# Choosing and weighting experts: look-up moved to four PSUM banks, four splits moved to GpSimd, one row split ahead, gate row by way of DRAM

## The chip, the core and the metric

The kernel runs on one core of one Trainium2 chip. A core has TensorE (PE, matrix products into PSUM), VectorE (DVE), ScalarE (ACT), GpSimd (POOL), and SyncE (SP), whose queue issues all DMAs here. SBUF and PSUM have 128 partitions; PSUM has eight banks of 512 float32 columns per partition. The metric is the device time of one execution in microseconds (us), as the median of several runs. The change touches the last quarter of the kernel alone.

## The reference, cut to what matters

The whole model is two blocks of norms, feed-forward layers, attention and convolution on 256 tokens of 1024 channels. The change lies in the last layer, which has 16384 experts, of which each token uses 8 heads x 16:

```python
q = (hblk @ w_q).reshape(B, TB, PEER_HEADS, 2, PEER_DHALF)
s = jnp.einsum('btphd,phnd->btphn', q, subkeys).astype(jnp.float32)
v, i = lax.top_k(s, PEER_TOPK)                      # 16 of 128 rows, 16 of 128 columns per head
cand = (v[..., 0, :, None] + v[..., 1, None, :]).reshape(..., PEER_TOPK * PEER_TOPK)
cidx = (i[..., 0, :, None] * PEER_NKEYS + i[..., 1, None, :]).reshape(...)
tv, tj = lax.top_k(cand, PEER_TOPK)                 # 16 of the 256 pairs
eidx = jnp.take_along_axis(cidx, tj, axis=-1)
w = jax.nn.softmax(tv, axis=-1)
a = jax.nn.gelu(jnp.einsum('btd,btpkd->btpk', hblk, w_down[eidx]))
out = jnp.einsum('btpk,btpkd->btd', w * a, w_up[eidx])
...
x = x + ga2 * out                                   # the gate ga2: one value per channel
return _rms_norm(x, g_norm_final)
```

## The kernel before

The kernel computes all 16384 experts densely, as 128 rows of 128 ("expert e" below is one such row: 128 experts). The *first product* of expert e multiplies `w_down`'s 1024 x 128 block with the 256 tokens, and its activation (a `gelu` on ScalarE) is the row `slots[e]`, 128 x 256. The chosen experts' weights multiply these rows, with zero for what was not chosen. The *second product* multiplies each row with `w_up`'s 128 x 1024 block and adds all of them up in four banks.

Every matrix is split into a high and a low half, and a product is three matmuls (high x high, low x high, high x low): 24 matmuls for an expert of the first product (lines 298 to 300, in `mm3`), 12 for one of the second (line 1859, in `up`). The halves of a weight block come from `Stream`: a DMA on SP into one of four `raw` buffers (`load`, line 232), then in `split` a copy on ScalarE that makes the high half (line 252), then a subtraction that makes the low half, on GpSimd (line 254) or on DVE (line 256). Which of the two is a list of labels; `wdn` (all blocks of the first product) is on GpSimd, `wup` (those of the second) on DVE. The halves lie in a ring of four buffers (`Hh`, `Hl`, `hl0`, `hl1` in the last layer), and a block is split three experts ahead, when PE is done with the buffer's last block. In the trace, `X` as the input of a split is a `raw` buffer too.

Each engine works through its own queue in the order in which the program was written; nothing is reordered. That order is a loop over experts in `peer`, in which DVE's work is put between experts:

- *First stage* (expert 0 to 44). `topk` is a generator; it searches the top 16 per head on DVE (`MAX8`, `FIND_INDEX8`, `MATCH_REPLACE8`), adds pairs into `cand`, searches again, and then looks up which rows and columns were chosen (lines 1806, 1809 and 1811: compare with an iota, multiply with the index, add up; for two halves of the index and two halves of the tokens, each on 128 x 2048 columns of SBUF). Each `yield` tells its cost, and the loop puts in one expert for each 2.3 of it. Two experts later PE transposes the result (line 1666), and DVE copies it to SBUF (line 1667).
- *Second stage* (expert 45 to 127). For each token DVE makes two one-hots (line 1688 for four tokens' rows, line 1692 for a token's columns and weights), and PE multiplies them into a 128 x 128 map of weights (line 1700) in one of the banks `wb`. `place` (lines 1709 and 1711) multiplies the map of four tokens into the rows that exist, and puts it where a row does not exist yet; a later row takes its weights from there (lines 1614 and 1615, on ScalarE and DVE). `token` puts the tokens between the matmuls, evenly over the experts left.
- *Second product* (`finish`). `prep(e)` splits `slots[e]` with ScalarE and DVE (`split2`, lines 324 and 325), two experts ahead. After expert 32 `ends` loads the residual and the final norm's factors into SBUF of used rows, and makes the gate a row on all partitions: four diagonal matrices on DVE (line 1849) for each half, a product with ones on PE (line 1850), a copy (line 1851). The last experts, the residual, the norm and the output follow.

Banks before: experts go around banks 4, 5, 0, 1, 2, 3 in the first stage and around 0 to 3 in the second, where bank 4 holds the iota and banks 5, 6, 7 are `wb`. `mod(2, 0, 5)` is the gate, 128 x 8 in SBUF.

Of the kernel before, what the change touches and what calls it, by code (L numbers as in the profile page):

```python
# [8 lines left out]
F32 = mybir.dt.float32  # L9
# [180 lines left out]
class Stream:  # L190
# [45 lines left out]
    def split(self, upto):  # L236
        nc = self.nc
        while self.done < min(upto, len(self.units)):
# [5 lines left out]
            if split:  # L244
# [7 lines left out]
                nc.scalar.activation(hl[:, 0, :n], raw[:, :n], AF.Copy)  # L252
                if i in (1, 2) or label[0] == "wdn" or (label[0] == "win2f" and label[1] > 7 or label[0] == "win2r" or label[:2] == ("winf", 1) and label[2] in (0, 4, 11) or label[0] == "wout2" and label[1] < 5):
# [33 lines left out]
class Build:  # L287
# [1289 lines left out]
    def peer(self, fb):  # L1577
# [8 lines left out]
        SELT = Xf[:, 0, :768].rearrange("p (a t) -> p a t", a=3)  # L1586
        con = pp.tile([P, P], F32, name="iota")
        self.SA = self.ctx.enter_context(tc.tile_pool(name="slota", bufs=1)).tile([P, NSA * S], F32, name="slotA")
        slots = [self.SA[:, e * S:(e + 1) * S] for e in range(NSA)]
# [27 lines left out]
        with tc.tile_pool(name="topk", bufs=1) as p:  # L1617
# [29 lines left out]
            nc.sync.dma_start(con, I["con2"][:, OFF2["iota"][0]:OFF2["iota"][0] + P])  # L1647
            top = self.topk(p, con, SC, SEL)
            e = 0
# [21 lines left out]
        slots += [slotB[:, j * S:(j + 1) * S] for j in range(P - 1 - NSA)] + [Xf[:, 0, 1792:2048]]  # L1671
        self.ring = [0, 1, 2, 3]
        io = self.bank[4][:, :P]
        nc.vector.tensor_copy(io, con)
        wb = [5, 6, 7]
        SAv = self.SA.rearrange("p (e t) -> p e t", t=S)
# [18 lines left out]
        def weight(t):  # L1695
            if t >= T:
                return
            oh = ohs.pop(t)
            o = self.bank[wb[t // 4 % 3]][:, t % 4 * P:(t % 4 + 1) * P]
            nc.tensor.matmul(o, firsts[t // 4][:, t % 4], oh, start=True, stop=True)  # L1700

        def place(g, e):

            bv = self.bank[wb[g % 3]].rearrange("p (t e) -> p e t", e=P)
            ts = slice(4 * g, 4 * g + 4)
# [24 lines left out]

        rest = None
        while e < P or tok[0] < T:
            g0 = tok[0] // 4
# [8 lines left out]
            for g in range(g0, tok[0] // 4):  # L1742
                if g >= 1:
                    place(g - 1, e)
                if g == T // 4 - 1:
                    place(g, e)
            if e < P:
                rest = gelu(e, o)
                e += 1
        if rest:  # L1750
            rest()

        self.finish(slots, xd, pp)

    def topk(self, p, iota, SC, SEL):
# [43 lines left out]
        yield 1.6  # L1799
        io = iota[:, :16].unsqueeze(1).broadcast_to((P, P, 16))  # L1800
        for a in range(2):
            for t in range(2):
                eq = cand[t]
                iv = i16f[t].rearrange("p (h a) n -> p h a n", a=2)
                flat = eq.rearrange("p h k n -> p (h k) n")
                nc.vector.tensor_tensor(flat, abf[t][:, a].rearrange("p h k -> p (h k)").unsqueeze(2).broadcast_to((P, P, 16)),
                                        io, OP.is_equal)
                yield 2.3
                nc.vector.tensor_tensor(eq, eq, iv[:, :, a].unsqueeze(2).broadcast_to((P, 8, 16, 16)), OP.mult)
                yield 2.3  # L1810
                nc.vector.tensor_reduce(SEL[:, a, t], flat, axis=AX.X, op=OP.add)
                yield 2.3
                if a == 0 and t == 0:
# [9 lines left out]

    def finish(self, slots, xd, pp):
        nc, I, W = self.nc, self.I, self.W
        acc = [[self.bank[4 + 2 * t + c] for c in range(2)] for t in range(2)]
        cs = {}
        Hx = self.Hh[:, 0].rearrange("p k t -> p (k t)")
        Hf4 = [Hx[:, j * 512:(j + 1) * 512] for j in range(4)]

        def prep(e):
            c = Hf4[e % 4].rearrange("p (a t) -> p a t", a=2)
            self.split2((c[:, 0], c[:, 1]), slots[e])
            cs[e] = c

        ga = self.mod(2, 0, 5)
# [3 lines left out]
        dgs = [SA[:, 5120 + j * P:5120 + (j + 1) * P] for j in range(4)]  # L1840
# [21 lines left out]
        LATE = 4  # L1862
        prep(0)
        prep(1)
# [46 lines left out]
```

## Time and profile before

| what | us |
|---|---|
| median of 3 runs (2712.96 to 2716.12) | 2714.16 |
| the profiled execution's own time | 2713.35 |
| its span, first to last instruction | 2711.6 |
| first stage and search, about 1915 to 2055 | 140 |
| second stage, about 2055 to 2340 | 285 |
| step to the second product, about 2340 to 2352 | 12 |
| second product, about 2352 to 2697 | 345 |
| norm and output, about 2697 to 2711.6 | 14.6 |

In the profile a row names line, engine, operation, output<-inputs (buffer numbers left out), size and count. A matmul's end is modelled, so that one of 0.28 us may be followed by the next after 0.12. "Idle before" is the time in which the engine stood still, with what ended it. A DMA-issuing instruction of SP shows when it was issued, not how long the transfer took.

### The profile page before, as it was taken

The numbers are of one execution on the slowest core, as the hardware profiler recorded it, in microseconds if no ns is written. First come the engines' busy times: TensorE is split into PE (matmuls) and PEld (weight loads), VectorE is DVE, ScalarE is ACT, GpSimd is POOL, SyncE is SP. The second block draws the span as 40 slices with busy tenths as digits, with TensorE's granted clock in tenths as the row PEclk, the third lists the DMA queues.
The fourth block names the chain that finished last, engine by engine and source line by source line (L and its number), as shares of the span: only waits on it lengthen the run. The fifth ranks groups of instructions, "written<-read, shape, count | busy, mean of one in ns | idle before, by whom it ended". The sixth has DMA issues, their size and how long they took to land. (4 is left out here: it accounts for less than half of the span.)

```text
span 2711.6 us, 40950 instructions
## 1 busy us (share of the span) xinstructions
PE 2634.5 (97%) x15907; PEld 2307.1 (85%) x15907; DVE 1740.6 (64%) x3393; ACT 1088.7 (40%) x1864; POOL 506.5 (19%) x284
## 2 busy tenths in 40 slices
PE   7999999999999999999998999889989999999998
PEld 5888888688888898888978999779989999888887
DVE  4877865657776565555556656775794566655555
ACT  4322234533222232222345445544444544454554
POOL 1000010120000010000121002331797666300000
PEclk9999999999999999999999999999999999999999
DMA  6665643225565545565344665524555454566564
GB/s 265 208 192 186 200 133 115 65 94 170 186 184 198 172 138 192 189 197 187 104 145 138 193 191 169 173 72 166 170 163 172 149 149 151 160 201 197 194 194 139
DMA packets 129188, 451.40 MB, mean 166 GB/s; under 512 B 15968, under 2 KB 21088, under 8 KB 127200
## 3 DMA queue, kind: packets, MB, share of 16 engines
q1 hardware_dynamic: 128992, 448.77, 51.5%
q8 instruction: 125, 2.05, 0.3%
q14 instruction: 71, 0.58, 0.1%
HBM read 446.35 MB, written 2.10 MB: 165 GB/s over the span
## 5 line engine op out<-in xcount | busy, mean ns | idle before, releaser
L298 PE MATMUL bank<-Hh,hl 128*128 128x256 f32 (+1 forms) x1944 | 656.7, 338 | 8.8 <-ACT Hh L681 4.5
L300 PE MATMUL bank<-Hh,hl 128*128 128x256 f32 (+1 forms) x1944 | 634.2, 326 | 3.9 <-POOL hl L254 3.9
L299 PE MATMUL bank<-Hl,hl 128*128 128x256 f32 (+1 forms) x1944 | 634.7, 326 | 1.4 <-DVE Hl L684 1.2
L252 ACT ACTIVATE hl<-raw 128x1024 fp32r<-128x1024 f32 (+1 forms) x401 | 410.8, 1040 | 279.8 <-DMA raw<-in_w_dram 88.3
L256 DVE TENSOR_TENSOR hl<-raw,hl 128x1024 fp32r<-128x1024 f32 (+1 forms) x316 | 380.9, 1215 | 180.2 <-ACT hl L252 179.5
L298 PEld LDWEIGHTS bank<-Hh,hl 128*128 128x128 f32 x1944 | 369.4, 190 | 51.7 <-issue 10.3
L300 PEld LDWEIGHTS bank<-Hh,hl 128*128 128x128 f32 x1944 | 369.1, 190 | 36.0 <-POOL hl L254 4.5
L299 PEld LDWEIGHTS bank<-Hl,hl 128*128 128x128 f32 x1944 | 369.6, 190 | 32.4 <-DVE Hl L684 2.7
L532 DVE SCALAR_TENSOR_TENSOR junk<-wm,cb 128x1024 bf16<-128x1024 f32 x272 | 332.1, 1221 | 16.3 <-ACT cb L538 7.1
L635 POOL TENSOR_TENSOR nacc<-nlast,nacc 128x256 f32<-128x256 f32 (+1 forms) x56 | 60.2, 1080 | 1328.8 <-issue 834.4
L254 POOL TENSOR_TENSOR hl<-raw,hl 128x1024 fp32r<-128x1024 f32 x85 | 209.8, 2473 | 146.3 <-ACT hl L252 135.0
L298 PE MATMUL bank<-G,hl 128*128 128x512 f32 (+1 forms) x673 | 227.3, 338 | 0.0
L299 PE MATMUL bank<-G,hl 128*128 128x512 f32 (+1 forms) x673 | 226.4, 336 | 0.0
L300 PE MATMUL bank<-G,hl 128*128 128x512 f32 (+1 forms) x673 | 226.4, 336 | 0.0
L324 ACT ACTIVATE G<-silu 128x512 fp32r<-128x512 f32 (+1 forms) x88 | 51.1, 580 | 417.3 <-DVE silu L820 417.3
L1859 PE MATMUL bank<-hl,Hh 128*128 128x512 f32 x768 | 179.4, 389 | 0.0
L298 PE MATMUL bank<-Hh,hm 128*128 128x512 f32 (+1 forms) x496 | 175.4, 354 | 0.0
L299 PE MATMUL bank<-Hl,hm 128*128 128x512 f32 (+1 forms) x496 | 175.1, 353 | 0.0
L300 PE MATMUL bank<-Hh,hm 128*128 128x512 f32 (+1 forms) x496 | 175.1, 353 | 0.0
L1859 PEld LDWEIGHTS bank<-hl,Hh 128*128 128x128 f32 x768 | 144.2, 188 | 30.0
L820 DVE TENSOR_TENSOR silu<-silu,bank 128x512 f32<-128x512 f32 (+1 forms) x88 | 54.6, 621 | 179.0 <-PE bank L300 177.0
L746 DVE SCALAR_TENSOR_TENSOR X<-bank,mall,X 128x256 f32<-128x256 f32 x192 | 84.5, 479 | 125.4 <-PE bank L300 125.2
(367 smaller groups left out, 5032.6 us busy)
## 6 DMA issues: line engine op xcount, KB each, us to landing
raw<-in_w_dram SPq DMA_DIRECT2D x208, 512.0 KB, 4.2
wm<-in_wmod_dram SPq DMA_DIRECT2D x128, 512.0 KB, 4.3
X<-in_wdn_dram SPq DMA_DIRECT2D x64, 512.0 KB, 3.6
raw<-in_wdn_dram SPq DMA_DIRECT2D x64, 512.0 KB, 3.6
X<-in_wup_dram SPq DMA_DIRECT2D x64, 512.0 KB, 3.5
raw<-in_wup_dram SPq DMA_DIRECT2D x64, 512.0 KB, 3.5
raw<-in_w_dram SPq DMA_DIRECT2D x64, 448.0 KB, 3.8
wm<-in_wada_dram SPq DMA_DIRECT2D x48, 512.0 KB, 4.7
```

The costliest lines, as they stand in the source:

```text
L252: nc.scalar.activation(hl[:, 0, :n], raw[:, :n], AF.Copy)
L254: nc.gpsimd.tensor_tensor(hl[:, 1, :n], raw[:, :n], hl[:, 0, :n].bitcast(F32), OP.subtract)
L256: nc.vector.tensor_tensor(hl[:, 1, :n], raw[:, :n], hl[:, 0, :n].bitcast(F32), OP.subtract)
L298: mm(o, wh, xh, start=start, stop=False)
L299: mm(o, wh, xl, start=False, stop=False)
L300: mm(o, wl, xh, start=False, stop=stop)
L324: nc.scalar.activation(dst[0], src, AF.Copy)
L532: nc.vector.scalar_tensor_tensor(junk, w, 1.0, self.cb[c], op0=OP.mult, op1=OP.mult, accum_out=o)
L635: self.nadd.tensor_tensor(acc, last, acc, OP.add)
L746: nc.vector.scalar_tensor_tensor(x, self.bank_(b, T, half), g[:, d:d + 1], x, op0=OP.mult, op1=OP.add)
L820: nc.vector.tensor_tensor(s, s, self.bank_(bb, T), OP.mult)
L1859: nc.tensor.matmul(acc[t][n], c[:, a, ts], u[:, b, n * 512:(n + 1) * 512], start=e == 0 and a + b == 0, stop=e == P - 1 and a == 1)
```

## The change

It is four edits of the last layer.

*Look-up.* The comparison, the product and the sum of the look-up work on four PSUM banks (4 to 7), 512 columns each, where they worked on a tile of 2048 columns in SBUF; the iota is copied into bank 3 ahead of the search instead of into bank 4 after it. From there on experts go around banks 0, 1, 2, and `wb` has four banks, 4 to 7. The costs told by `yield` are 2.8 instead of 2.3.

*Splits.* The low halves of `wup` 0 to 3 go to GpSimd.

*First row.* A tile `zero` of its own takes the halves of `slots[0]`; `sides` makes them in the second stage, as soon as all tokens are placed.

*Gate.* At the layer's start the gate is written to DRAM in the order of channels; `ends` reads it back as one row on all partitions. The diagonal matrices and their products are gone.

```diff
-                if i in (1, 2) or label[0] == "wdn" or (label[0] == "win2f" ...
+                if i in (1, 2) or label[0] == "wdn" or label[0] == "wup" and label[1] < 4 or (label[0] == "win2f" ...
                     nc.gpsimd.tensor_tensor(hl[:, 1, :n], raw[:, :n], hl[:, 0, :n].bitcast(F32), OP.subtract)
...
+        zero = pp.tile([P, 512], F32R, name="zero")
+        self.gd = tc.dram_tile([1, D], F32, name="gd")
+        nc.sync.dma_start(self.gd.rearrange("o (j p) -> p (o j)", p=P), self.mod(2, 0, 5))
...
             nc.sync.dma_start(con, I["con2"][:, OFF2["iota"][0]:OFF2["iota"][0] + P])
-            top = self.topk(p, con, SC, SEL)
+            self.ring = [0, 1, 2]
+            io = self.bank[3][:, :P]
+            nc.vector.tensor_copy(io, con)
+            top = self.topk(p, io, SC, SEL)
...
-        self.ring = [0, 1, 2, 3]
-        io = self.bank[4][:, :P]
-        nc.vector.tensor_copy(io, con)
-        wb = [5, 6, 7]
+        wb = [4, 5, 6, 7]
...
+            if tok[0] == T and not early and rest is None and e > NSA:
+                early = [self.sides(zero, slots[0])]
...
         for a in range(2):
             for t in range(2):
-                eq = cand[t]
                 iv = i16f[t].rearrange("p (h a) n -> p h a n", a=2)
-                flat = eq.rearrange("p h k n -> p (h k) n")
-                nc.vector.tensor_tensor(flat, abf[t][:, a]...unsqueeze(2).broadcast_to((P, P, 16)), io, OP.is_equal)
-                yield 2.3
-                nc.vector.tensor_tensor(eq, eq, iv[:, :, a].unsqueeze(2).broadcast_to((P, 8, 16, 16)), OP.mult)
-                yield 2.3
-                nc.vector.tensor_reduce(SEL[:, a, t], flat, axis=AX.X, op=OP.add)
-                yield 2.3
+                eqs = [self.bank[4 + b] for b in range(4)]
+                flat = [eq.rearrange("p (k n) -> p k n", n=16) for eq in eqs]
+                for b in range(4):
+                    mine = abf[t][:, a, 2 * b:2 * b + 2].rearrange("p h k -> p (h k)")
+                    nc.vector.tensor_tensor(flat[b], mine.unsqueeze(2).broadcast_to((P, 32, 16)), io, OP.is_equal)
+                yield 2.8
+                for b in range(4):
+                    q = eqs[b].rearrange("p (h k n) -> p h k n", h=2, k=16)
+                    nc.vector.tensor_tensor(q, q, iv[:, 2 * b:2 * b + 2, a].unsqueeze(2).broadcast_to((P, 2, 16, 16)), OP.mult)
+                yield 2.8
+                for b in range(4):
+                    nc.vector.tensor_reduce(SEL[:, a, t, 32 * b:32 * b + 32], flat[b], axis=AX.X, op=OP.add)
+                yield 2.8
...
+    def sides(self, c, slot):
+        c = c.rearrange("p (a t) -> p a t", a=2)
+        self.split2((c[:, 0], c[:, 1]), slot)
+        return c
...
             nc.sync.dma_start(gf, I["gfin"].broadcast_to((P, D)))
-            for n in range(2):
-                b = self.bank[n]
-                for j in range(4):
-                    nc.vector.tensor_scalar(dgs[j], self.C["ident"], ga[:, 4 * n + j:4 * n + j + 1], None, op0=OP.mult)
-                    nc.tensor.matmul(b[:, j * P:(j + 1) * P], self.C["ones"], dgs[j], start=True, stop=True)
-                nc.vector.tensor_copy(gab[:, n * 512:(n + 1) * 512], b)
+            nc.sync.dma_start(gab, self.gd.broadcast_to((P, D)))
...
-        prep(0)
+        if not early:
+            prep(0)
```

The first place is DVE's queue in the look-up, where one pass (one half of the index, one half of the tokens) stands. Before, it and the next pass (`cand`, `abf` and `i16f` are tiles of SBUF):

```order
L1806 TENSOR_TENSOR cand_14971<-abf_14979,iota 128x2048
L1809 TENSOR_TENSOR cand_14971<-cand_14971,i16f_14969 128x2048
L1811 TENSOR_REDUCE SEL<-cand_14971 128x128
L1806 TENSOR_TENSOR cand_14972<-abf_14980,iota 128x2048
L1809 TENSOR_TENSOR cand_14972<-cand_14972,i16f_14970 128x2048
L1811 TENSOR_REDUCE SEL<-cand_14972 128x128
```

Now the same pass, with banks 3 (`bank_66`) and 4 to 7 (`bank_67` to `bank_70`):

```order
L1814 TENSOR_TENSOR bank_67<-abf_14983,bank_66 128x512
L1814 TENSOR_TENSOR bank_68<-abf_14983,bank_66 128x512
L1814 TENSOR_TENSOR bank_69<-abf_14983,bank_66 128x512
L1814 TENSOR_TENSOR bank_70<-abf_14983,bank_66 128x512
L1818 TENSOR_TENSOR bank_67<-bank_67,i16f_14973 128x512
L1818 TENSOR_TENSOR bank_68<-bank_68,i16f_14973 128x512
L1818 TENSOR_TENSOR bank_69<-bank_69,i16f_14973 128x512
L1818 TENSOR_TENSOR bank_70<-bank_70,i16f_14973 128x512
L1821 TENSOR_REDUCE SEL<-bank_67 128x32
L1821 TENSOR_REDUCE SEL<-bank_68 128x32
L1821 TENSOR_REDUCE SEL<-bank_69 128x32
L1821 TENSOR_REDUCE SEL<-bank_70 128x32
```

Three operations of four times the columns have become twelve, and none has two inputs in SBUF any more.

The second place is DVE's queue at the end of the second stage. Before, from the first split of the second product (line 256) to the first row's halves:

```order
L256 TENSOR_TENSOR Hh<-X,Hh 128x1024
L1688 TENSOR_TENSOR X<-bank_67,X 128x512
L1692 TENSOR_SCALAR oh<-bank_67,X 128x128 x3
L1615 TENSOR_TENSOR slotB<-bank_66,slotB 128x244
L1709 TENSOR_TENSOR slotA<-slotA,bank_69 128x68x4
L1709 TENSOR_TENSOR slotB<-slotB,bank_69 128x57x4
L256 TENSOR_TENSOR Hl<-X,Hl 128x1024
L1692 TENSOR_SCALAR oh<-bank_67,X 128x128
...
L256 TENSOR_TENSOR hl_77<-raw_75,hl_77 128x1024
L1615 TENSOR_TENSOR slotB<-bank_64,slotB 128x256
L1615 TENSOR_TENSOR X<-bank_65,X 128x256
L325 TENSOR_TENSOR Hh<-slotA,Hh 128x256 x2
```

Now, from the last products of weights with rows on:

```order
L1618 TENSOR_TENSOR slotB<-bank_65,slotB 128x248
L1712 TENSOR_TENSOR slotA<-slotA,bank_69 128x68x4
L1712 TENSOR_TENSOR slotB<-slotB,bank_69 128x58x4
L1712 TENSOR_TENSOR slotA<-slotA,bank_70 128x68x4
L1712 TENSOR_TENSOR slotB<-slotB,bank_70 128x58x4
L325 TENSOR_TENSOR zero<-slotA,zero 128x256
L1618 TENSOR_TENSOR slotB<-bank_63,slotB 128x256
L1618 TENSOR_TENSOR X<-bank_64,X 128x256
L325 TENSOR_TENSOR Hh<-slotA,Hh 128x256 x2
L256 TENSOR_TENSOR Hh<-X,Hh 128x1024
```

The splits of line 256 are gone from between the one-hots, the first row's half stands ahead of the activations of the last two experts, and the first split on DVE is that of `wup` 4.

On PE the order has 48 matmuls more ahead of the transposes of the look-up's result, so two experts have moved from the second stage to the first.

## Rows read from the trace of the kernel before

**Rows 1.** Busy time by stage: stretch; PE, PEld, DVE, ACT, POOL; clock; DMA share; GB/s.

```profile
1915.00:2055.00 140.00, 133.06 (x1107) 131.42 (x1108) 119.90 (x420) 66.98 (x97) 129.77 (x45) 1.00 0.56 169
...
2055.00:2340.00 285.00, 284.40 (x2435) 284.23 (x2434) 174.37 (x500) 141.29 (x376) 191.51 (x80) 1.00 0.49 150
...
2352.00:2438.00 86.00, 86.00 (x381) 71.20 (x380) 49.67 (x64) 42.38 (x62) 0.00 (x0) 1.00 0.61 194
```

**Rows 2.** Timeline of ScalarE: start, duration, line, operation [idle before]; three of 45 activations.

```profile
1976.74 0.38 ACT L1611 ACTIVATE slotA<-bank 128x256 f32<-128x256 f32 x1 [0.73 <-PE bank L300]
...
1999.46 0.38 ACT L1611 ACTIVATE slotA<-bank 128x256 f32<-128x256 f32 x1 [1.54 <-PE bank L300]
...
2033.82 0.39 ACT L1611 ACTIVATE slotA<-bank 128x256 f32<-128x256 f32 x1 [2.70 <-PE bank L300]
```

**Rows 3.** Timeline of GpSimd beside the look-up.

```profile
2008.54 2.39 POOL L254 TENSOR_TENSOR Hh<-X,Hh 128x1024 fp32r<-128x1024 f32 x1
...
2010.90 4.43 POOL L254 TENSOR_TENSOR Hl<-X,Hl 128x1024 fp32r<-128x1024 f32 x1
...
2030.80 4.81 POOL L254 TENSOR_TENSOR hl<-raw,hl 128x1024 fp32r<-128x1024 f32 x2
```

**Rows 4.** Timeline of VectorE from the look-up to the copies of its result.

```profile
1990.76 2.27 DVE L1806 TENSOR_TENSOR cand<-abf,iota 128x2048 f32<-128x2048 f32 x1
...
1993.07 4.39 DVE L1809 TENSOR_TENSOR cand<-cand,i16f 128x2048 f32<-128x2048 f32 x1
...
2008.59 4.50 DVE L1806 TENSOR_TENSOR cand<-abf,iota 128x2048 f32<-128x2048 f32 x1
...
2031.46 4.29 DVE L1821 TENSOR_TENSOR SEL<-SEL,ss 128x128 f32<-128x128 f32 x2
...
2053.95 1.09 DVE L1667 COPY X<-bank 128x256 f32<-128x256 f32 x3 [18.20 <-PE bank L1666]
```

**Rows 5.** Groups of instructions by form, 2056 to 2352 (count, busy us, mean ns, idle before).

```profile
L254 POOL TENSOR_TENSOR hl<-raw,hl 128x1024 fp32r<-128x1024 f32 x40 | 95.8, 2396 | 44.7 <-ACT hl L252 38.4 <-PE bank L300 6.3
...
L252 ACT ACTIVATE hl<-raw 128x1024 fp32r<-128x1024 f32 x42 | 44.2, 1052 | 0.0
...
L1688 DVE TENSOR_TENSOR X<-bank,X 128x512 f32<-128x512 f32 x63 | 43.6, 692 | 88.7 <-PE bank L1700 88.7
```

**Rows 6.** Timelines of VectorE and TensorE at the step to the second product.

```profile
2339.00 1.23 DVE L256 TENSOR_TENSOR Hh<-X,Hh 128x1024 fp32r<-128x1024 f32 x1 [3.45 <-ACT Hh L252]
...
2344.35 0.28 PE L300 MATMUL bank<-Hh,hl 128*128 128x256 f32 x1
...
2346.08 0.49 PE L1700 MATMUL bank<-oh,X 128*128 128x128 f32 x2 [1.45 <-DVE oh L1692]
...
2350.16 1.19 PE L1859 MATMUL bank<-Hh 128*128 128x512 f32 x4 [0.78 <-ACT Hh L324]
...
2351.54 2.11 PE L1859 MATMUL bank<-Hh 128*128 128x512 f32 x8 [0.19 <-DVE Hh L325]
```

**Rows 7.** Timeline of TensorE around the gate's row.

```profile
2437.80 2.88 PE L1859 MATMUL bank<-Hh 128*128 128x512 f32 x12
...
2443.96 3.00 PE L1859 MATMUL bank<-Hl,Hh 128*128 128x512 f32 x12
```

**Rows 8.** Timeline of SP's queue at the layer's start and after expert 32.

```profile
1849.09 5.93 SPq L232 DMA_DIRECT2D raw<-in_wpq_dram  x2
...
1871.29 0.33 SPq L1626 DMA_DIRECT2D subk<-in_subk_dram  x1
...
2435.77 1.12 SPq L1845 DMA_DIRECT2D slotA<-in_gfin_dram  x1
```

**Rows 9.** Who waited for whom, 2352 to 2712: total us, times, longest.

```profile
ACT hl L252 <- PE bank L1859: 83.9, 62, 1.4
```

**Rows 10.** Timelines of VectorE and TensorE around expert 118's row and expert 121.

```profile
2319.18 0.38 DVE L1615 TENSOR_TENSOR slotB<-bank,slotB 128x224 f32<-128x224 f32 x1
...
2323.35 0.36 PE L298 MATMUL bank<-Hh,Hl 128*128 128x256 f32 x1
```

More of the change, by code (lines that the diff above doesn't have):

```diff
@@ L252, in split @@
                 nc.scalar.activation(hl[:, 0, :n], raw[:, :n], AF.Copy)
-                if i in (1, 2) or label[0] == "wdn" or (label[0] == "win2f" and label[1] > 7 or label[0] == "win2r" or label[:2] == ("winf", 1) and label[2] in (0, 4, 11) or label[0] == "wout2" and label[1] < 5):
+                if i in (1, 2) or label[0] == "wdn" or label[0] == "wup" and label[1] < 4 or (label[0] == "win2f" and label[1] > 7 or label[0] == "win2r" or label[:2] == ("winf", 1) and label[2] in (0, 4, 11) or label[0] == "wout2" and label[1] < 5):
                     nc.gpsimd.tensor_tensor(hl[:, 1, :n], raw[:, :n], hl[:, 0, :n].bitcast(F32), OP.subtract)
@@ L1698, in weight @@
             oh = ohs.pop(t)
-            o = self.bank[wb[t // 4 % 3]][:, t % 4 * P:(t % 4 + 1) * P]
+            o = self.bank[wb[t // 4 % 4]][:, t % 4 * P:(t % 4 + 1) * P]
             nc.tensor.matmul(o, firsts[t // 4][:, t % 4], oh, start=True, stop=True)
         def place(g, e):
-            bv = self.bank[wb[g % 3]].rearrange("p (t e) -> p e t", e=P)
+            bv = self.bank[wb[g % 4]].rearrange("p (t e) -> p e t", e=P)
             ts = slice(4 * g, 4 * g + 4)
@@ L1731, in peer @@
         rest = None
+        early = []
         while e < P or tok[0] < T:
@@ L1751, in peer @@
             rest()
-        self.finish(slots, xd, pp)
+        self.finish(slots, xd, early)
     def topk(self, p, iota, SC, SEL):
@@ L1799, in topk @@
         yield 1.6
-        io = iota[:, :16].unsqueeze(1).broadcast_to((P, P, 16))
+        io = iota[:, :16].unsqueeze(1).broadcast_to((P, 32, 16))
         for a in range(2):
             for t in range(2):
-                eq = cand[t]
                 iv = i16f[t].rearrange("p (h a) n -> p h a n", a=2)
-                flat = eq.rearrange("p h k n -> p (h k) n")
-                nc.vector.tensor_tensor(flat, abf[t][:, a].rearrange("p h k -> p (h k)").unsqueeze(2).broadcast_to((P, P, 16)),
-                                        io, OP.is_equal)
-                yield 2.3
-                nc.vector.tensor_tensor(eq, eq, iv[:, :, a].unsqueeze(2).broadcast_to((P, 8, 16, 16)), OP.mult)
-                yield 2.3
-                nc.vector.tensor_reduce(SEL[:, a, t], flat, axis=AX.X, op=OP.add)
-                yield 2.3
+                eqs = [self.bank[4 + b] for b in range(4)]
[11 more added lines that the diff above has]
+                yield 2.8
                 if a == 0 and t == 0:
@@ L1822, in topk, with finish @@
         yield 1.2
-    def finish(self, slots, xd, pp):
+    def sides(self, c, slot):
+        c = c.rearrange("p (a t) -> p a t", a=2)
+        self.split2((c[:, 0], c[:, 1]), slot)
+        return c
+    def finish(self, slots, xd, early):
         nc, I, W = self.nc, self.I, self.W
         acc = [[self.bank[4 + 2 * t + c] for c in range(2)] for t in range(2)]
-        cs = {}
+        cs = dict(enumerate(early))
         Hx = self.Hh[:, 0].rearrange("p k t -> p (k t)")
@@ L1831, in prep @@
         def prep(e):
[L1832 to L1836, printed above, removed]
+            cs[e] = self.sides(Hf4[e % 4], slots[e])
         SA = self.SA
@@ L1839, in finish @@
         gf, gab, tmp = [SA[:, j * 1024:(j + 1) * 1024] for j in range(2, 5)]
-        dgs = [SA[:, 5120 + j * P:5120 + (j + 1) * P] for j in range(4)]
         def ends():
```

## The prediction

> **What bounds the kernel now.** I read the busy time by stage first. TensorE (PE) runs at clock 1.00 in the experts' part and is busy for all of it except in a few places, so a microsecond is won only where PE stands still: 7 us of idle time in the first stage of 140 us, next to nothing in the second of 285 us, none in the second product [rows 1]. Then I looked for those places.
>
> Place 1 is the look-up. An expert's activation on ScalarE starts as PE ends it, so these starts give PE's pace: from 1976.74 to 1999.46 eight experts, 2.84 us each; from 1999.46 to 2033.82 nine, where 9 x 2.84 = 25.6 would do [rows 2]. **8.8 us** go there. The reason stands in GpSimd's and VectorE's (DVE's) rows: a split of one half on GpSimd takes 2.4 us alone and 4.4 where DVE has a look-up operation beside it [rows 3], and DVE's own operation takes 2.27 once and 4.4 to 4.5 elsewhere [rows 4]. At 2008.54 GpSimd runs at its own pace while DVE's comparison of 2008.59 lasts 4.50; at 2010.90 it is GpSimd that waits. They take turns, and a split at 4.4 us is slower than PE's 2.84.
>
> Place 2 is the step from the first product to the second. DVE waits 3.45 us for ScalarE with the first split of the second product at 2339.00, with one-hots queued behind it, and PE waits 1.45 us for a one-hot at 2346.08, then 0.78 and 0.19 for the first row's two halves [rows 6]. PE's matmul before 2346.08 began at 2344.35, and one follows another every 2.84/24 = 0.12 us, so the first wait cost 1.6. A matmul lasts 0.28, so a stall hides 0.16 more than its idle time shows: 0.78 + 0.19 + 2 x 0.16 = 1.3. Together **2.9 us**.
>
> Place 3 is the gate's row, made on PE with eight products between experts 32 and 33 of the second product: the first matmul of 33 starts at 2443.96, that of 32 at 2437.80 [rows 7], 6.16 us apart. The stage's own pace is 86.00/381 x 12 = 2.71 [rows 1]. **3.4 us**.
>
> **The change part by part.** *Look-up in banks.* Twelve operations on 2048 columns become 48 on 512 columns in four PSUM banks, each with one SBUF input at most. The nearest row is the second stage's product of a bank with a row of SBUF, 512 columns, 692 ns (63 of them), beside which GpSimd's 40 splits ran at 2396 ns [rows 5]: neither held up the other. At that price the look-up takes 48 x 0.69 = 33 us and touches GpSimd nowhere. It starts at 1990.76 plus 0.28 for the copy of the iota, now ahead of the search, so it ends near 2024; the closing weights have two SBUF inputs still (4.29 for two, [rows 4]) and end DVE near 2030. PE wants the result after the first stage, which has two experts more (the steps' costs in the code rise by 12 x 0.5 in units of 2.3, and the order has 48 matmuls more ahead of the transposes): 2053.6 - 8.8 + 2 x 2.84 = 2050.5. DVE waited 18.2 us there [rows 4] and would wait 20. The two experts cost nothing; they leave the second stage, whose 256 tokens are shared by 80 experts instead of 82. GpSimd at 2.4 per split and PE at 2.84 per expert: I take the whole 8.8. Bounds: nothing, if these operations still lock GpSimd out; 8.8 at most.
>
> *Iota.* The copy leaves the chain between the transposes and the first one-hot; 0.3 us, at least 0. Its new place is behind a DMA that landed before DVE came there.
>
> *Three banks for experts, four for weights.* The tightest case I found in the second stage: DVE's product of expert 118 from its bank starts at 2319.18 and takes 0.38, and the third expert after it starts at 2323.35 [rows 10]. With three banks that expert would need this very bank, 3.8 us after it is free. Cost 0.
>
> *First splits on GpSimd, first row early.* Four DVE operations of 1.23 leave the end of the second stage, so the one-hots no longer wait behind ScalarE, and the first row is split while expert 127 runs on PE. GpSimd has no split left there but these; each is wanted some 8 us after its buffer is free, and takes 1.05 on ScalarE and 2.4 [rows 5]. That should give back 2.9. But the row splits have two SBUF inputs on DVE. ScalarE does the last placements, the early row's half (0.4), an activation (0.39) and the copy (1.05) between expert 126's end and the third GpSimd split, which therefore runs for 2.4 us from about where expert 127 ends. The second row's DVE half, 0.42 us, is ready about 0.9 us into that and gets its turn as GpSimd's split ends, near 2.9 us after expert 127's end, where PE wants it after 2.71. Cost 0.3 us; between 0 and 2.4 (one GpSimd operation more).
>
> *Gate through DRAM.* The write of 1024 single words is issued into SP's idle stretch between its work that ends at 1855.0 and 1871.29 [rows 8]; no row shows such a write, its cost lies between 0 and what exceeds 16 us, and I take 0. The read is 0.5 MB more beside experts 30 to 34. It is a broadcast like the final norm's row, which kept SP for 1.12 us [rows 8]. In the stage before, 194 GB/s took 0.61 of the DMA engines [rows 1], so 0.5 MB takes about 1.7 us of all. The pause of PE that covered the burst goes too: loads come up to 3.4 + 1.7 = 5.1 us later against their use. ScalarE's copies wait for PE's buffers all through, not for a DMA [rows 9], and a copy is due three experts ahead, 8.1 us, of which it and DVE need 1.05 + 1.23: 5.8 us of cover, over and above what a load has. Cost 0; if the cover failed, up to 3.4.
>
> **Sum**: 8.8 + 0.3 + (2.9 - 0.3) + 3.4 = 15.1 us. The profiled execution took 2713.35 (span 2711.6 and 1.7 around it), 0.8 below the median of 2714.16; the median becomes **2699.0**.
>
> **The rivals.** *1. GpSimd holds DVE up at the step.* The rows have the case: two small products of 2031.46 took 4.29 us, since each waited for a whole GpSimd operation [rows 3, 4]. If the third or fourth split gets its turn first, the second row comes one GpSimd operation later, 2.4 - 0.3 = 2.1 us more: 2701. For it: the order of two waiting engines is not in my hands. Against it: there DVE, waiting since 2031.46, got its turn as the first of the two GpSimd operations ended.
> The Trainium skill speaks against this part of the change in "SBUF — State Buffer", section "Who interferes with whom": a VectorE instruction with two SBUF inputs and a GpSimd one that reads SBUF exclude each other for the whole instruction, and the one that came first goes on. By that rule a waiting row split loses up to a whole GpSimd operation; the trace agrees (4.29 us for two products that move 128 columns).
>
> *2. The DMA burst shows.* Without PE's pause the loads come late and PE stops near experts 33 to 36: up to 3.4 back, 2702.4. Against it is the cover of 5.8 us.
>
> *3. The look-up still locks GpSimd out*, because of the one SBUF input or the SBUF output that is left, so the change doesn't do there what its words say: 8.8 back, 2707.8. Against it are the rows of 692 and 2396 ns.
>
> *4. Slower: the ring of three banks.* If DVE's products came later than the third expert's start, PE would wait in each of 80 experts. To lose more than the 15.1 it takes 0.19 us per expert, which needs products that come 4 us later than in the tightest case of before; if they came 4.1 later, 80 x 0.3 = 24 us would go: 2723. Against it: DVE is busy for 174 of 285 us there [rows 1], so lateness doesn't pile up from expert to expert.
>
> **How the numbers follow.** Forecast 0.70; rival 1 0.13, rival 2 0.05, rival 3 0.07, rival 4 0.05. About 0.2% (5.4 us) is what a measurement of this kernel can tell from no change. The forecast and rivals 1 and 2 are faster by more; rival 3 lies on that border (2708.7), so 0.02 of it goes to faster and 0.05 to the same; rival 4 is slower. Faster 0.90, same 0.05, slower 0.05. Range: below, all bounds at their best (8.8 + 0.3 + 2.9 + 3.4 = 15.4) and the runs' own spread and the rough ends of the three stalls, 3 us: 2696; above, rivals 1 and 2 together: 2699.0 + 2.1 + 3.4 = 2704.5, taken as 2705. Rivals 3 and 4 stay outside.
>
> **What would show it.** Right: GpSimd's splits at 2.4 us through the look-up, the experts' activations 2.84 us apart up to the transposes, DVE's look-up operations at about 0.69; PE without a wait for a one-hot at the end of the second stage and under half a microsecond before the second row; experts 32 and 33 of the second product 2.71 apart. Wrong: splits of over 4 us beside the look-up; a DVE row split of over 2 us at the step; ScalarE waiting for a DMA near expert 35; a PE wait on ScalarE's or DVE's product between experts of the second stage.

## The result, and the profile after

The changed kernel takes 2700.16 us (median of 4 runs, 2698.27 to 2702.59), the kernel before 2713.56 in the same comparison (4 runs, 2712.86 to 2716.12): ratio 0.9945, 95% interval 0.9933 to 0.9957. Forecast were 2699.0 and a range of 2696 to 2705. The profiled execution took 2698.27, its span is 2696.5.

In the tables below, the *layer* is the stretch from the first matmul of expert 0 to the last of the second product, read off TensorE's timeline. It went from 786.06 us (1916.57 to 2702.63) to 770.0 (1917.69 to 2687.72): **16.0 us**. The layer began 1.1 us later, in code that the change doesn't touch, and the norm and output behind it are 0.2 shorter, so the span is 15.1 shorter.

The busy time of the changed kernel by stage (columns as in [rows 1]; the third stretch begins and ends 2 us earlier here):

```profile
1915.00:2055.00 140.00, 139.32 (x1171) 138.63 (x1172) 119.47 (x464) 68.61 (x102) 118.89 (x48) 1.00 0.58 182
2055.00:2340.00 285.00, 285.00 (x2440) 284.91 (x2439) 180.08 (x507) 142.57 (x383) 189.78 (x81) 1.00 0.47 149
2350.00:2436.00 86.00, 86.00 (x381) 71.19 (x381) 48.84 (x64) 42.35 (x62) 0.00 (x0) 1.00 0.67 216
```

In the first stage PE is busy for 139.32 of 140 us, where it was for 133.06 [rows 1]. ScalarE's timeline, three of the experts' activations, answers to [rows 2]:

```profile
1977.63 0.38 ACT L1614 ACTIVATE slotA<-bank 128x256 f32<-128x256 f32 x1 [1.54 <-PE bank L300]
...
2000.36 0.38 ACT L1614 ACTIVATE slotA<-bank 128x256 f32<-128x256 f32 x1 [1.54 <-PE bank L300]
...
2034.43 0.38 ACT L1614 ACTIVATE slotA<-bank 128x256 f32<-128x256 f32 x1 [1.54 <-PE bank L300]
```

Eight experts in 22.73 us and then twelve in 34.07: 2.84 each, through the whole look-up. GpSimd beside it [rows 3] and DVE from the search's end to the copies [rows 4]:

```profile
2001.76 2.50 POOL L254 TENSOR_TENSOR Hh<-X,Hh 128x1024 fp32r<-128x1024 f32 x1 [0.31 <-ACT Hh L252]
2004.64 2.42 POOL L254 TENSOR_TENSOR Hl<-X,Hl 128x1024 fp32r<-128x1024 f32 x1 [0.38 <-ACT Hl L252]
```

```profile
1997.19 1.39 DVE L1797 TENSOR_SCALAR ab<-tj 128x128 uint32<-128x128 uint32 x1
...
1998.91 2.69 DVE L1800 CAST abf<-ab 128x256 f32<-128x256 uint32 x2
...
2001.93 2.48 DVE L1814 TENSOR_TENSOR bank<-abf,bank 128x512 f32<-128x512 f32 x4
2004.32 2.48 DVE L1818 TENSOR_TENSOR bank<-bank,i16f 128x512 f32<-128x512 f32 x4
...
2051.76 1.12 DVE L1673 COPY X<-bank 128x256 f32<-128x256 f32 x3 [18.84 <-PE bank L1672]
```

Splits at 2.4 to 2.5 us, four look-up operations in 2.48, and DVE still waits 18.84 us for the transposes. At the step to the second product [rows 6], first DVE and GpSimd, then PE:

```profile
2340.33 4.39 DVE L325 TENSOR_TENSOR Hh<-slotA,Hh 128x256 fp32r<-128x256 f32 x2
```

```profile
2339.49 4.96 POOL L254 TENSOR_TENSOR hl<-raw,hl 128x1024 fp32r<-128x1024 f32 x2 [2.39 <-ACT hl L252]
```

```profile
2339.39 2.89 PE L1866 MATMUL bank<-Hh,zero 128*128 128x512 f32 x12
2342.12 2.88 PE L1866 MATMUL bank<-Hl,Hh 128*128 128x512 f32 x12
...
2426.44 2.88 PE L1866 MATMUL bank<-Hh 128*128 128x512 f32 x12
2429.16 2.88 PE L1866 MATMUL bank<-Hl,Hh 128*128 128x512 f32 x12
```

PE goes from the last expert into the second product with no wait. The second row's and the third row's halves on DVE each waited for GpSimd, 4.39 us for two, and were done in time: the second row's at 2342.18, where the second expert starts at 2342.12 but needs this half only at its fifth matmul, 0.9 us later. The last two rows are the places of experts 32 and 33 [rows 7]: 2.72 apart, where they were 6.16. ScalarE was held up there once, which it was not before:

```profile
2436.44 1.06 ACT L252 ACTIVATE hl<-raw 128x1024 fp32r<-128x1024 f32 x1 [2.99 <-DMA raw<-in_wup_dram]
```

### The profile page after: what moved, and what is told of

The parts are those of the page before. It is cut to its first block, busy times and chain, and to the rows that moved or that the text cites. A ratio compares the mean times of both kernels' runs of the same rounds, so it can differ in the third digit from the quotient of the medians.

```text
span 2696.5 us, 40877 instructions
## 1 busy us (share of the span) xinstructions
PE 2630.2 (98%) x15891; PEld 2304.6 (85%) x15891; DVE 1735.6 (64%) x3414; ACT 1087.0 (40%) x1861; POOL 499.5 (19%) x288
```

## The experiments

The theory: GpSimd's splits and those operations of VectorE that read two SBUF tensors exclude each other for a whole operation, and this made the look-up cost 8.8 us; the step and the gate are separate gains of 3.3 and 3.4. The rivals: what helped the look-up was the output in PSUM, or the shorter operations; the step's two edits are one; the DMA burst or the ring of three banks takes something back.

The times of whole runs are too coarse for this. The layer starts anywhere from 1915.9 to 1923.6 us in kernels whose code ahead of it is the same (the start of expert 0 in the table), so the parts are compared by the layer's own length, read off one profiled execution of each kernel; in five of the kernels below it is the same to 0.01 us. Each ratio is to the kernel before in the same comparison, whose median was 2715.21 us for undo_lookup, undo_step, undo_gate and rope_both and 2716.25 for rope_columns.

| kernel | run time, us | ratio to before, 95% | layer starts | layer, us | against changed |
|---|---|---|---|---|---|
| before | 2713.56 | | 1916.57 | 786.06 | +16.0 |
| changed | 2700.16 | 0.9945 (0.9933 to 0.9957) | 1917.69 | 770.04 | |
| undo_lookup | 2708.24 | 0.9976 (0.9964 to 0.9987) | 1922.87 | 777.08 | +7.04 |
| undo_step | 2700.34 | 0.9949 (0.9932 to 0.9966) | 1915.91 | 773.34 | +3.30 |
| undo_gate | 2701.41 | 0.9955 (0.9938 to 0.9971) | 1917.19 | 773.60 | +3.56 |
| lookup_operand | 2698.36, one run | | 1917.70 | 770.04 | 0.00 |
| lookup_pieces | 2718.69, one run | | 1922.19 | 785.96 | +15.92 |
| undo_split | 2703.89, one run | | 1921.55 | 771.78 | +1.74 |
| undo_early | 2704.27, one run | | 1921.97 | 771.74 | +1.70 |
| two_banks | 2696.88, one run | | 1915.86 | 770.49 | +0.45 |
| all_gpsimd | 2700.85, one run | | 1920.27 | 770.04 | 0.00 |
| burst | 2706.71, one run | | 1923.63 | 772.00 | +1.96 |
| rope_both | 2694.71 | 0.9927 (0.9910 to 0.9943) | 1907.65 | 770.04 | 0.00 |
| rope_columns | 2690.50 | 0.9901 (0.9885 to 0.9918) | 1910.16 | 770.04 | 0.00 |

### Each part undone

*The look-up back in SBUF.*

```diff
-            top = self.topk(p, io, SC, SEL)
+            top = self.topk(p, con, SC, SEL)
...
+                eq = cand[t]
+                flat = eq.rearrange("p h k n -> p (h k) n")
+                nc.vector.tensor_tensor(flat, abf[t][:, a]...unsqueeze(2).broadcast_to((P, P, 16)), io, OP.is_equal)
+                yield 2.3
+                nc.vector.tensor_tensor(eq, eq, iv[:, :, a].unsqueeze(2).broadcast_to((P, 8, 16, 16)), OP.mult)
```

> The changed kernel with its look-up put back on the 2048 columns of SBUF (iota from SBUF too, the old step costs, so two experts go back to the second stage); rows, splits and gate as changed. Theory: GpSimd's splits and DVE's products with two SBUF inputs take turns again, splits of 4.4 to 4.8 us beside the look-up, PE's pace lost in nine experts, 8.8 us: 2700.2 + 8.8 = 2709 us. Rival, that the gain of this stage came from the two experts that moved or from the banks of the experts: splits of 4.4 us or not, the experts stay 2.84 us apart, and the time is within 1 us of 2700.

GpSimd and DVE in this kernel's look-up:

```profile
2013.83 8.98 POOL L254 TENSOR_TENSOR hl<-raw,hl 128x1024 fp32r<-128x1024 f32 x2
2022.77 4.43 POOL L254 TENSOR_TENSOR Hh<-X,Hh 128x1024 fp32r<-128x1024 f32 x1
```

```profile
2007.12 4.49 DVE L1812 TENSOR_TENSOR cand<-abf,iota 128x2048 f32<-128x2048 f32 x1
2011.64 4.37 DVE L1815 TENSOR_TENSOR cand<-cand,i16f 128x2048 f32<-128x2048 f32 x1
2016.05 2.29 DVE L1817 TENSOR_REDUCE SEL<-cand 128x128 f32<-128x2048 f32 x1
```

The long splits and the long products are back; the sum, which reads one tensor, stays at 2.29. The experts lose 7.04 us and not 8.8: the price depends on how splits and products happen to meet. The rival falls as far as the banks go: the experts still go around three of them and lose their pace. The two experts move back with the look-up here; lookup_pieces below leaves them where the change has them, and loses as well.

*The step.*

```diff
-                if i in (1, 2) or label[0] == "wdn" or label[0] == "wup" and label[1] < 4 or (label[0] == "win2f" ...
+                if i in (1, 2) or label[0] == "wdn" or (label[0] == "win2f" ...
...
-            if tok[0] == T and not early and rest is None and e > NSA:
-                early = [self.sides(zero, slots[0])]
```

> The changed kernel without the early row and with the first four splits of the second product on DVE again. Theory: the three waits of PE at the step are back (1.45, 0.78 and 0.19 us of idle time, 2.9 to 3.3 us of its pace): 2703.3 us. Rival, that the step was made faster by the fourth bank of weights or by the two experts that moved: under 1 us, and PE shows no wait for a one-hot.

The layer is 3.30 us longer, as the theory has it. The run time is not (2700.34): in the profiled execution this kernel's layer started 1.8 us earlier.

One edit at a time, first the splits back on DVE (the first place of the diff alone), then no early row (the second alone):

> The changed kernel with the first four splits of the second product on DVE again; the first row stays early. Theory: the one-hots queue behind DVE's wait for ScalarE, PE waits about 1.5 us for one near the end of the second stage (1.6 lost), and the first row makes none wait: span 1.6 us longer. Rival, that the early row alone does it all: no wait for a one-hot, nothing lost.

> The changed kernel without the early row; the first four splits stay on GpSimd. Theory: PE waits for the first row, 1.3 us as before at least, and DVE's row splits, six of 0.42 us with two SBUF inputs, wait for GpSimd's splits of 2.4: up to 2.4 more, span 1.3 to 3.7 us longer, more than the early row's share of the 3.2. Rival, that GpSimd doesn't hold DVE up at the step: 1.3 us, DVE's row splits at 0.42.

PE's waits in the one and in the other:

```profile
2341.84 0.49 PE L1703 MATMUL bank<-oh,X 128*128 128x128 f32 x2 [1.45 <-DVE oh L1695]
```

```profile
2344.61 1.19 PE L1864 MATMUL bank<-Hh 128*128 128x512 f32 x4 [0.78 <-ACT Hh L324]
2346.18 2.09 PE L1864 MATMUL bank<-Hh 128*128 128x512 f32 x8 [0.37 <-DVE Hh L325]
```

The waits of [rows 6] return one by one: 1.45 for the one-hot with the splits, 0.78 and 0.37 (0.19 before) for the first row. They cost 1.74 and 1.70, together 3.44 against 3.30 for both, so the edits add up. In the second kernel DVE's three row splits take 4.37 us beside GpSimd's, and the first of them keeps PE 0.18 longer than before; a whole GpSimd operation, which the expectation allowed for, was not lost.

*The gate made on PE.*

```diff
-            nc.sync.dma_start(gab, self.gd.broadcast_to((P, D)))
+            for n in range(2):
+                b = self.bank[n]
+                for j in range(4):
+                    nc.vector.tensor_scalar(dgs[j], self.C["ident"], ga[:, 4 * n + j:4 * n + j + 1], None, op0=OP.mult)
+                    nc.tensor.matmul(b[:, j * P:(j + 1) * P], self.C["ones"], dgs[j], start=True, stop=True)
+                nc.vector.tensor_copy(gab[:, n * 512:(n + 1) * 512], b)
```

> The changed kernel with the gate's row made on PE from diagonal matrices again, nothing written to DRAM. Theory: experts 32 and 33 of the second product 6.1 us apart instead of 2.72, all of it lost: 2703.6 us. Rival, that the read through DRAM costs something later (ScalarE waited 3.0 us for a DMA in the changed kernel): then this kernel loses less than 2.5 us, and some later expert of the second product is nearer to its neighbour here than in the changed kernel.

PE around expert 32:

```profile
2425.95 2.88 PE L1871 MATMUL bank<-Hh 128*128 128x512 f32 x12
2429.05 1.16 PE L1862 MATMUL bank<-slotA,con 128*128 128x128 f32 x8 [0.22 <-DVE slotA L1861]
2431.19 1.16 PE L1862 MATMUL bank<-slotA,con 128*128 128x128 f32 x8 [0.98 <-DVE slotA L1861]
2432.10 3.01 PE L1871 MATMUL bank<-Hl,Hh 128*128 128x512 f32 x12
```

6.15 us from 2425.95 to 2432.10, and 3.56 longer in all; no later expert gets anything back. The DMA way is free here.

### What frees the look-up

> The changed kernel with the look-up in SBUF again, 2048 columns to an operation, written to SBUF; only the smaller input (the iota, and the index, copied there as floats) lies in a PSUM bank. The step costs stay at 2.8. So each operation has one SBUF input, but is as long as before and writes SBUF. Theory (two SBUF inputs are what excludes GpSimd): splits at 2.4 us, look-up operations at about 2.2 us, experts 2.84 us apart, span as of the changed kernel, 2696.5 within 2 us. Rival, that it was the output in PSUM or the shortness of the operations: splits of over 4 us, 8 to 9 us lost.

```diff
+        i16f = [self.bank[4][:, t * 256:(t + 1) * 256].rearrange("p (a n) -> p a n", a=16) for t in range(2)]
...
+                eq = cand[t]
                 iv = i16f[t].rearrange("p (h a) n -> p h a n", a=2)
-                eqs = [self.bank[4 + b] for b in range(4)]
-                flat = [eq.rearrange("p (k n) -> p k n", n=16) for eq in eqs]
...
+                flat = eq.rearrange("p h k n -> p (h k) n")
+                nc.vector.tensor_tensor(flat, abf[t][:, a]...unsqueeze(2).broadcast_to((P, P, 16)), io, OP.is_equal)
```

DVE in this kernel's look-up, and GpSimd beside it:

```profile
2001.38 2.27 DVE L1813 TENSOR_TENSOR cand<-abf,bank 128x2048 f32<-128x2048 f32 x1
...
2006.01 2.29 DVE L1818 TENSOR_REDUCE SEL<-cand 128x128 f32<-128x2048 f32 x1
```

```profile
2001.78 2.41 POOL L254 TENSOR_TENSOR Hh<-X,Hh 128x1024 fp32r<-128x1024 f32 x1 [0.47 <-ACT Hh L252]
```

Long operations that write SBUF, and neither engine holds up the other: the layer is as long as in the changed kernel, to 0.01 us. For these operations what matters is the second SBUF input. Twelve operations do what 48 do in the change.

> The changed kernel with the look-up on SBUF alone, but in the same 48 operations of 512 columns. Theory: each of the 32 products has two SBUF inputs and waits for a whole GpSimd operation, so it takes 2.4 us and more, and GpSimd waits 0.6 for each: DVE needs 32 x 2.9 = 93 us where it needed 20, has 19 us to spare before the transposes, and PE stands still for 54 us there: span near 2750. Rival, that short operations are what helped: products of 0.6 to 0.7 us, PE loses less than 3 us.

```diff
-                eqs = [self.bank[4 + b] for b in range(4)]
+                eqs = [cand[t][:, 2 * b:2 * b + 2].rearrange("p h k n -> p (h k n)") for b in range(4)]
```

DVE, then GpSimd, then who waited for whom from 1915 to 2075:

```profile
2006.44 11.31 DVE L1814 TENSOR_TENSOR cand<-abf,iota 128x512 f32<-128x512 f32 x4
...
2024.67 2.48 DVE L1814 TENSOR_TENSOR cand<-abf,iota 128x512 f32<-128x512 f32 x4
2027.07 2.48 DVE L1818 TENSOR_TENSOR cand<-cand,i16f 128x512 f32<-128x512 f32 x4
...
2031.86 11.27 DVE L1814 TENSOR_TENSOR cand<-abf,iota 128x512 f32<-128x512 f32 x4
```

```profile
2024.98 9.16 POOL L254 TENSOR_TENSOR hl<-raw,hl 128x1024 fp32r<-128x1024 f32 x2 [0.24 <-ACT hl L252]
```

```profile
PEld bank L1672 <- DVE SEL L1821: 13.0, 1, 13.0
```

Short operations don't help: four of them take 11.3 us, 2.8 each, where the same four with one SBUF input take 2.48, and PE waits 13 us at the transposes. But the loss is 15.9 us, not 54. Where GpSimd stood idle as DVE's products came (2024.67), eight of them went through one behind another in 4.9 us and GpSimd's split waited for them all; where a product met a running split (2031.86), the two took turns. My expectation had turns throughout. Why the turns don't begin as soon as GpSimd wants its split at 2024.98 is open.

### The reserves: banks, GpSimd, DMA

> The changed kernel with experts going around banks 0 and 1 in place of 0, 1, 2. In the changed kernel's trace DVE's product of expert 117 ends at 2307.04 and the second expert after it starts at 2308.00, about the tightest. Theory (three banks cost nothing, with 4.4 us to spare): even two cost nothing, 0.95 us to spare, span within 1 us of 2696.5. Rival, that the banks are near a limit: a wait of PE on ScalarE's or DVE's product in most of 79 experts, 0.3 us each, 24 us lost.

```diff
-            self.ring = [0, 1, 2]
+            self.ring = [0, 1]
```

0.45 us, all of it at the transposes, which go through the ring too; from the transposes to the step no expert is later. Not even the ring of two is near its limit, and rival 4 falls.

> The changed kernel with 64 more splits of the second product (blocks 4 to 67) on GpSimd. Theory: DVE's two row halves per expert (0.42 us, two SBUF inputs each) and GpSimd's split of 2.4 exclude each other, 2.4 + 0.84 = 3.24 us per expert against PE's 2.72: 64 x 0.52 = 33 us lost, row halves of 2 us and more. Rival, that they do not: 2.4 us fit into 2.72, nothing lost, row halves of 0.42.

```diff
-                if i in (1, 2) or label[0] == "wdn" or label[0] == "wup" and label[1] < 4 or (label[0] == "win2f" ...
+                if i in (1, 2) or label[0] == "wdn" or label[0] == "wup" and label[1] < 68 or (label[0] == "win2f" ...
```

The group of DVE's row halves from 2343 to 2520 (count, busy, mean ns, idle before), then one split and the row half beside it:

```profile
L325 DVE TENSOR_TENSOR Hh<-slotA,Hh 128x256 fp32r<-128x256 f32 x66 | 161.2, 2460 | 16.0 <-ACT Hh L324 15.8
```

```profile
2397.77 2.40 POOL L254 TENSOR_TENSOR hl<-raw,hl 128x1024 fp32r<-128x1024 f32 x1 [0.32 <-ACT hl L252]
2400.49 2.40 POOL L254 TENSOR_TENSOR Hh<-X,Hh 128x1024 fp32r<-128x1024 f32 x1 [0.32 <-ACT Hh L252]
```

```profile
2398.03 2.42 DVE L325 TENSOR_TENSOR Hh<-slotA,Hh 128x256 fp32r<-128x256 f32 x1 [0.30 <-ACT Hh L324]
```

The mechanism is there in every expert: the row half takes 2460 ns in the mean, 0.42 alone. The 33 us were wrong twice over: DVE has one row half per expert, not two (ScalarE makes the other), and it needs only 0.28 us behind the split (2400.45 against 2400.17), which fits into GpSimd's gap of 0.32. PE loses nothing, with 0.04 us to spare.

> The changed kernel with three more reads of the gate's row (0.5 MB each, into used rows of SBUF) behind the one after expert 32. Theory: 3 x 1.7 = 5.1 us more of transfers, so ScalarE's wait for a load goes from 3.0 to about 8 us; the cover is 5.8 us, and PE stands still for about 2.3 us between experts 34 and 38. Rival, that the loads catch up in the share of the DMA engines that is free: no wait of PE.

```diff
             nc.sync.dma_start(gab, self.gd.broadcast_to((P, D)))
+            for j in range(3):
+                nc.sync.dma_start(SA[:, (5 + j) * 1024:(6 + j) * 1024], self.gd.broadcast_to((P, D)))
```

ScalarE, DVE and PE:

```profile
2446.01 1.06 ACT L252 ACTIVATE hl<-raw 128x1024 fp32r<-128x1024 f32 x1 [6.61 <-DMA raw<-in_wup_dram]
2446.97 0.40 ACT L324 ACTIVATE Hh<-slotA 128x256 fp32r<-128x256 f32 x1
```

```profile
2448.24 0.42 DVE L325 TENSOR_TENSOR Hh<-slotA,Hh 128x256 fp32r<-128x256 f32 x1
```

```profile
2443.27 2.88 PE L1868 MATMUL bank<-Hh 128*128 128x512 f32 x12
2447.42 3.41 PE L1868 MATMUL bank<-Hl,Hh 128*128 128x512 f32 x12 [1.27 <-ACT Hh L324]
```

PE loses 1.96 us, near the 2.3 expected, but for another reason. It doesn't wait for the late weights. It waits for a row's half that stands behind the late copy in ScalarE's queue (2446.97, done at 2447.37) and is due two experts ahead, not three. ScalarE waits 1.35 us for PE before every copy anyway, so the copy came 6.61 - 1.35 = 5.3 us late; the expert that follows starts 4.15 us after the one before, 1.4 over the pace. Then it waits once more, for the same row's half on DVE (done at 2448.66), and takes 3.24 instead of 2.72. The cover was 5.3 - 1.4 = **3.9 us** for ScalarE's half and 5.3 - 2.0 = **3.3 us** for both, where the prediction took 5.8. In the changed kernel the copy was 2.99 - 1.35 = 1.6 late, well inside.

### The same cure elsewhere

> The changed kernel, and the same cure at another place, the rotation in the attention block before: the product with the sine stays in its PSUM bank and the sum reads it there, the product with the cosine reads the bank in place of ScalarE's copy; neither has two SBUF inputs then. Theory: the sums RQ and RK, four of which took 2.14 to 2.15 us on the chain that ended last (0.42 elsewhere), and the product of 2.59 us take about 0.42, 4 x 1.7 + 2.2 = 9 us at most, of which something else that is late may take back half: 2691 to 2696 us. Rival, that these operations waited for something other than GpSimd, or that PE has another late input there: within 1 us of 2700.

```diff
-                    nc.vector.tensor_tensor(src, src, C["cos" + kind], OP.mult)
-                    tmp = p.tile([P, T], F32, name="rtmp", tag="rtmp", bufs=2)
-                    nc.vector.tensor_tensor(tmp, o, C["sin" + kind], OP.mult)
-                    nc.vector.tensor_tensor(dst, src, tmp, OP.add)
+                    nc.vector.scalar_tensor_tensor(src, self.bank[b][:, :T], scale, C["cos" + kind], op0=OP.mult, op1=OP.mult)
+                    nc.vector.tensor_tensor(o, o, C["sin" + kind], OP.mult)
+                    nc.vector.tensor_tensor(dst, src, o, OP.add)
```

The group of the sums RQ from 1735 to 1845, in the changed kernel and in this one:

```profile
L1205 DVE TENSOR_TENSOR RQ<-rsrc,rtmp 128x256 f32<-128x256 f32 x4 | 8.6, 2150 | 0.1
```

```profile
L1204 DVE TENSOR_TENSOR RQ<-rsrc,bank 128x256 f32<-128x256 f32 x4 | 1.7, 422 | 0.1
```

ScalarE's copies of weights, compared one by one with those of the changed kernel, come 0.02 us earlier at 1662.43 and 9.85 us earlier at 1843.86: 9.8 us won in this stretch, a little more than the 9 expected at most. This compares two single executions, each the fastest of its kernel's four. The medians differ by less: 2694.71 us (2688.26 to 2696.34) against 2700.16, so 5.5.

In this kernel a further operation stood out that reads one tensor only, and two columns of it: it ended with GpSimd's split (a pair from 1746.11 on) whenever it met one.

```profile
1744.61 0.17 DVE L1449 TENSOR_SCALAR nst<-nst 128x2 f32<-128x2 f32 x1
...
1748.56 2.31 DVE L1449 TENSOR_SCALAR nst<-nst 128x2 f32<-128x2 f32 x1
```

> The kernel with the rotation in banks (rope_both), and the softmax's change of sign, a 128x2 operation with a single SBUF input, made as two operations of 128x1. In rope_both eight of its 16 executions lay beside a GpSimd split and each ended with that split (2.31, 2.17, 0.95, 0.70, 0.70, 0.70, 0.66 and 0.28 us against 0.17 alone), though only one input is read. Theory (a single-input operation is excluded too where VectorE runs it in a mode that takes two columns at a time, as the Trainium skill's page on advanced engine details lists it for even sizes; a single column cannot): all 32 operations take about 0.17 us beside GpSimd, 7 us of waits go, 16 x 0.1 = 1.6 us come, and of these about half lie on the path: the layer after it starts 1 to 4 us earlier against the projections ahead of this stretch. Rival, that any operation of this kind waits for GpSimd whatever its size: operations of 0.7 to 2.3 us remain, and the layer starts 0 to 2 us later.

```diff
-            nc.vector.tensor_scalar(st[:, 2:4], st[:, 0:2], -1.0, None, op0=OP.mult)
+            for b in range(2):
+                nc.vector.tensor_scalar(st[:, 2 + b:3 + b], st[:, b:b + 1], -1.0, None, op0=OP.mult)
```

The group of these operations from 1720 to 1840, then a GpSimd pair with two of them inside it:

```profile
L1450 DVE TENSOR_SCALAR nst<-nst 128x1 f32<-128x1 f32 x32 | 4.3, 151 | 0.0
```

```profile
1749.65 4.73 POOL L254 TENSOR_TENSOR hl<-raw,hl 128x1024 fp32r<-128x1024 f32 x2 [6.19 <-ACT hl L252]
```

```profile
1753.68 0.27 DVE L1450 TENSOR_SCALAR nst<-nst 128x1 f32<-128x1 f32 x2
```

All 32 take 151 ns in the mean, where 16 took 614; 18 of the 32 lie wholly inside a split, and none waited. So the waits are gone, but a gain in time is not shown. Against the copies of weights of rope_both the layer comes 1.1 us earlier from 1662 on, the low end of what was expected; yet over this same stretch the twelve kernels here whose code in the attention block is that of before differ by almost 4 us. The 2690.50 us of this kernel is the lowest median here, and what its distance from rope_both's 2694.71 consists of stays open.

## Why the prediction was right

*Look-up, 8.8 us: right.* The splits, the pace of 2.84 and the place of the cure are as told, and undo_lookup and lookup_operand show the reason: two SBUF inputs. The price of 0.69 per operation was a little high: they follow one another every 0.60, 28.7 us in all instead of 33. Wrong was its start, 2001.93 instead of 1991. Of these 11 us, 1.1 are the layer's later start. The largest part, 6.5, was lost ahead of the second search, where DVE casts the indices and adds the pairs (a sum with two SBUF inputs). VectorE's timeline, before and now:

```profile
1955.25 0.27 DVE L1782 CAST i16f<-i 128x256 f32<-128x256 uint32 x1
```

```profile
1956.56 2.32 DVE L1788 CAST i16f<-i 128x256 f32<-128x256 uint32 x1
...
1963.41 4.49 DVE L1790 TENSOR_TENSOR cand<-v 128x2048 f32<-128x2048 f32 x1
```

Before, the cast began 0.04 us after a GpSimd split and went ahead of it, and that split took 7.17 us; now it began 0.24 us after one and waited. A further 3.4 went at the integer shifts and casts behind the search (1.39 us, and 2.69 for two), which waited for GpSimd though they read one tensor. I had reckoned with such waits in the look-up, its closing weights and the row splits alone. They cost nothing, since DVE still had 18.84 us to spare. The Trainium skill names both kinds, operations with two SBUF inputs and casts or operations with a scalar, in "SBUF — State Buffer", section "Who interferes with whom": the latter can take GpSimd's ports as well; the rows agree (0.17 alone and 2.31 beside a split for two columns). The Trainium skill's "Advanced Engine Details and Errata", section "VectorE Performance Modes", lists as a condition of the mode with two read ports that the outermost sizes be even, or odd, equal and above one; a single column took 0.15 beside a split.

*Iota, 0.3: right.* The two experts that hold the transposes took 3.77 + 3.73 us, before 3.51 + 4.38: 0.39.

*Step, 2.9 less 0.3: too small.* It was 3.3 (undo_step). Two terms were off. The stalls of before sum to 3.3: the experts around them took 5.34, 3.83 and 3.33 where 3.62, 2.89 and 2.73 is the pace now, against my 1.6 + 1.3 from the idle time and the overlap of a matmul. And the second row cost nothing, not 0.3: it did wait for GpSimd, as forecast, and was done 2.8 us after expert 127's end, against the 2.9 forecast. But I had PE want it at the expert's start, and PE needs DVE's half only at the fifth matmul, 0.9 us later ([rows 6] show it: four matmuls, then the wait for DVE). Rival 1's lost turn of 2.1 us would by this have cost about 1.2, an estimate; DVE got its turn first, as in the case that spoke against this rival.

*Banks, 0: right*, by two_banks with room to spare.

*Gate, 3.4: right* (3.56 by undo_gate), *the cover of the DMA burst wrong.* I listed ScalarE's wait for a DMA as a sign against the forecast, and it came (2.99 us), yet PE lost nothing. The step that failed is "a copy is due three experts ahead, 5.8 us of cover": the row's halves behind the copy are due earlier, and burst measured 3.9 for ScalarE's and 3.3 for both. The write of single words, which I priced at nothing, took SP 0.43 us and landed 10.6 us after its issue, all of it in SP's idle stretch.

*Sum.* The layer gained 16.0, not 15.1: 8.8 + 0.4 + 3.3 + 3.4 = 15.9. The profiled execution gained exactly the 15.1 forecast because its layer also started 1.1 later; that part is luck. The medians, 2713.56 and 2700.16, differ by 13.4. The three parts undone sum to 7.04 + 3.30 + 3.56 = 13.9; of the 2.1 that lack, 1.8 is the look-up, whose price depends on how the engines meet, and 0.3 the iota, which undo_lookup leaves in its new place.

## What to carry to other kernels

Look through the trace for VectorE operations whose time is their own plus a piece of a GpSimd operation: with a second SBUF input they waited for the whole of it here, and GpSimd for them, and casts and operations with a scalar on two columns or more waited too. Moving one of two inputs to PSUM was enough; cutting the operation up made it worse (15.9 us lost against 7.0). Before pricing such a wait, look for who needs the result next: 66 waits of 2 us cost nothing where GpSimd's own gap took them, and the turns in the look-up cost 8.8 us where PE stood behind them.

## What the runs showed that I had not expected

- An operation on 128x2 that takes 0.17 us alone took 2.31 beside a split; two on 128x1 took 0.15 each. Why a single column is let through, no run here shows beyond that.
- Turns are not the only pattern: eight short products with two SBUF inputs ran for 4.9 us in a row while GpSimd's split waited (9.16 us for a pair of splits), while in other stretches of the same loop each product waited for a split.
- The layer took the same time to 0.01 us in five kernels, and yet layers started up to 8 us apart in kernels with the same code ahead of them, which is more than any of the three parts measured here. Where it arises can be read off ScalarE's copies of weights, compared one by one: the distances of these kernels are the same at 300 and at 1250 us, to 0.2; they come up ahead of 300 us and change between 1300 and 1850, near 1400 by up to 4 us. Why is open.
